# Parameter rows on GpSimd's queue, and the first quarter of scale multiplied between the transposes of x

## The chip, the core and the metric

The program runs on one core of one Trainium2 chip. The metric is the device time of one execution in microseconds (us); lower is better. TensorE (PE) multiplies, VectorE (DVE), ScalarE (ACT) and GpSimd (POOL) work on tiles, and SyncE (SP) only asks for transfers. ACT and GpSimd can ask for transfers too. Each engine works through its own list of instructions in order and waits on semaphores for the others.

## The reference

One layer of a flow-matching backbone on 512 latent tokens and 128 context tokens, 2048 wide, all in float32. What matters here is its beginning:

```python
sh1, sc1, g1, sh2, sc2, g2 = jnp.split(mod, 6, axis=-1)      # mod = silu(c) @ w_mod + b_mod
h = _rmsnorm(x, lp['norm1_g']) * (1.0 + sc1) + sh1
p = h @ lp['w_in']
o_a, s_fin = _rwkv7_bidir(shift_fn(p[..., :C_SHIFT], lp['mu_shift']), s0, lp)
o_b = _chunk_gmlp(jax.nn.gelu(p[..., C_SHIFT:]), lp)
x = x + g1 * (jnp.concatenate([o_a, o_b], axis=-1) @ lp['w_out'])
h = _rmsnorm(x, lp['norm2_g']) * (1.0 + sc2) + sh2
ff = (jax.nn.silu(h @ lp['w_ffn_gate']) * (h @ lp['w_ffn_up'])) @ lp['w_ffn_down']
return x + g2 * ff, s_fin
```

`mod` is computed for two conditioning vectors (latent and context) with w_mod of 2048 x 12288. `_rwkv7_bidir` reads small parameter vectors: mu_shift, w0, a0, k_k, k_a, r_k, gn_w and gn_b. After the layer comes a last RMSNorm.

## The kernel before

The 640 tokens stand as 5 tiles of 128 rows. The program has an opening of some 149 us, which makes the normalized and modulated h for all tokens, and then the main part: the rest of h @ w_in with the recurrence, w_out, the feed-forward products and the last norm. Only the opening's code is touched.

In the opening, each tile of x (`xall`) is squared and summed on ACT; GpSimd takes the reciprocal root `rs` (line 135); DVE scales the tile by it (line 242); TensorE transposes it in 16 blocks into the PSUM tile `ptx` (line 246); DVE and ACT copy it to `xnT` (line 247). TensorE's list is written out by hand in this stretch: its instructions stand in the order of the Python code. The other engines' lists are ordered by a scheduler from the same code.

Then come four rounds j = 0 to 3. Round j makes 512 columns of scale (g = 1) and 512 of shift (g = 0) of `mod`, each by `quarter(g, j)`. A quarter fetches four pieces of w_mod of 1 MB (`wt`, line 304, asked for by SyncE) and multiplies each with the conditioning vectors (`cT`, line 308, into `pm`, four products a piece; the trace counts each of them twice). Counted through all rounds, the pieces are called wt0 to wt31 here: wt0 to wt3 are the first quarter of scale. There are five buffers for them, so a piece can be asked for only when the product of the piece five before it is done. After the fourth piece ACT copies `pm` to `ms` (line 312), TensorE transposes `ms` in four blocks (`ptm`, line 316), and DVE reduces this to `mc`. After both quarters DVE makes `hf` (line 342) of four blocks of h, and splits it into `h_hi` and `h_lo` (lines 344 and 345). Between the pieces of the next round stand the first products of h with three column blocks of w_in (`products(j)`, lines 188 to 190, into `big`), whose weights are fetched as `raw` (line 165) and split into `hi` and `lo`.

```python
for j in range(4):
    for i, _ in enumerate(itertools.chain(quarter(1, j), quarter(0, j))):
        if i in (2, 3, 4, 6, 7, 8):
            next(prods, None)
    ...
    prods = products(j)
    if j == 1:
        rows()
    if j == 2:
        params()
```

`rows()` (lines 263 to 278) asks for 20 small transfers, of 128 bytes to 12 KB each, that put the parameter vectors as rows into `rowA` and `rowB`. `params()` (lines 280 to 286) transposes both on TensorE and copies the columns into `prm`, which the main part reads. `rowC` holds b_mod and norm1_g; ACT asks for it, and its transposition `pp` (line 250) gives `bmod` (line 252).

SyncE's list of the transfers follows the code. Besides the buffers, a transfer also waits for the landing of the one that was asked for eight before it on its kind of queue: SyncE and ACT share eight such lanes, called DMAHW0 to DMAHW7 in the lists of waits, and GpSimd has eight of its own, DMASW0 to DMASW7.

Of the kernel before, what the change touches and what calls it, by code (L numbers as in the profile page):

```python
# [22 lines left out]
T = 640  # L23
NT = T // P
HALF = T // 2
# [11 lines left out]
RMS_EPS = 1e-6  # L37
# [18 lines left out]
ROWO = 4  # L56
RAWB = 13
FRONT = 4
REST = 6
LATE = 2  # L60
OFF = 13
# [19 lines left out]
NPRM = 212  # L81
# [6 lines left out]
def flow_step(ctx: ExitStack, tc, x_prompt, x_sample, state_rwkv, c, c_ctx, w_mod, b_mod,  # L88
# [3 lines left out]
    nc = tc.nc  # L92
    V, S, G, TE = nc.vector, nc.scalar, nc.gpsimd, nc.tensor
# [19 lines left out]
    ident = cp.tile([P, P], F32, name="ident")  # L113
    make_identity(nc, ident)
    I2 = cb.tile([P, CH], F32, name="I2")
    for h in range(2):
# [8 lines left out]
                         op0=ALU.mult, op1=ALU.add)  # L125
# [8 lines left out]
    def rsqrt(out, in_):  # L134
        return G.tensor_tensor(out=out, in0=in_, in1=mhalf.to_broadcast(list(in_.shape)), op=ALU.pow)

    prm = cp.tile([P, NPRM], F32, name="prm")
# [57 lines left out]
    hpool = hp.enter_context(tc.tile_pool(name="hpool", bufs=1))  # L195
    junk = hpool.tile([P, D], F32, tag="h_hi", name="junk")
    xall = hpool.tile([P, NT, D], F32, tag="h_lo", name="xall")


    pmx, pex, pbx = ExitStack(), ExitStack(), ExitStack()  # L200
    pm_ = pmx.enter_context(tc.tile_pool(name="pm_", bufs=1, space=PSUM))
    ptE = pex.enter_context(tc.tile_pool(name="ptE", bufs=1, space=PSUM))
    FIRST = (3072, 3200, 3328)
    with ExitStack() as ph:
        ph.enter_context(tc.manual_schedule(engines={mybir.EngineType.PE}))
        p0 = ph.enter_context(tc.tile_pool(name="p0", bufs=1))
# [24 lines left out]
        V.tensor_copy(cT3[:, :, 1], pc[:, 0, 16:32])  # L231


        xnT = p0.tile([P, KB, T], F32, name="xnT")
        for t in range(NT):
            xt = xall[:, t, :]
            ss = p0b.tile([P, 1], F32, name="ss")
            S.activation(junk, xt, AF.Square, accum_out=ss)
            V.tensor_scalar(ss, ss, 1.0 / D, RMS_EPS, op0=ALU.mult, op1=ALU.add)
            rs = p0b.tile([P, 1], F32, name="rs")  # L240
            rsqrt(rs, ss)
            V.tensor_scalar_mul(xt, xt, rs[:, 0:1])
            for q in range(4):
                pt = ps0.tile([P, 4, P], F32, tag="pt", name="ptx")
                for b in range(4):
                    TE.transpose(pt[:, b, :], xt[:, (4 * q + b) * P:(4 * q + b + 1) * P], ident)
                (S.copy if q % 2 else V.tensor_copy)(xnT[:, 4 * q:4 * q + 4, t * P:(t + 1) * P], pt)

        pp = ps0.tile([P, 4, P], F32, tag="pt", name="pp")
        TE.transpose(pp[:, 0, 0:48], rowC, ident[0:48, 0:48])  # L250
        bmod = p0.tile([P, 2, KB], F32, name="bmod")
# [1 line left out]
        V.tensor_scalar_add(bmod[:, 1, :], bmod[:, 1, :], 1.0)  # L253
        V.tensor_copy(prm[:, C_N1:C_N2], pp[:, 0, 32:48])


        rowA = p0.tile([P, P], F32, name="rowA")
        rowB = p0.tile([P, P], F32, name="rowB")
        G.memset(rowB, 0.0)
        G.memset(rowA, 0.0)  # L260
        nA = C_W0

        def rows():
            for m in range(4):
                nc.sync.dma_start(rowA[C_MU + 24 * m:C_MU + 24 * m + 24, :],
                                  mu_shift[0, m, 0:3072].rearrange("(r p) -> r p", p=P))
                nc.sync.dma_start(rowA[C_MU2 + 2 * m:C_MU2 + 2 * m + 2, :],
                                  mu_shift[0, m, 3072:3328].rearrange("(r p) -> r p", p=P))
                nc.sync.dma_start(rowA[C_MU3 + m:C_MU3 + m + 1, 0:32], mu_shift[0, m:m + 1, 3328:3360])
            for off, src in ((C_W0, w0[0].rearrange("d (r p) -> (d r) p", p=P)),  # L270
                             (C_A0, a0[0].rearrange("d (r p) -> (d r) p", p=P)),
                             (C_KK, k_k[0].rearrange("(r p) -> r p", p=P)),
                             (C_KA, k_a[0].rearrange("(r p) -> r p", p=P)),
                             (C_RK, r_k[0].rearrange("(r h) n -> r (h n)", h=2)),
                             (C_GW, gn_w[0].rearrange("(r h) n -> r (h n)", h=2)),
                             (C_GB, gn_b[0].rearrange("(r h) n -> r (h n)", h=2)),
                             (C_N2, norm2_g[0].rearrange("(r p) -> r p", p=P))):
                nc.sync.dma_start(rowB[off - nA:off - nA + src.shape[0], :], src)

        def params():  # L280
            pp = ptE.tile([P, 4, P], F32, tag="ptE", name="pp")
            TE.transpose(pp[:, 0, :], rowA, ident)
            TE.transpose(pp[:, 1, :], rowB, ident)
            V.tensor_copy(prm[:, 0:nA], pp[:, 0, 0:nA])
            V.tensor_copy(prm[:, nA:C_N1], pp[:, 1, 0:C_N1 - nA])
            V.tensor_copy(prm[:, C_N2:NPRM], pp[:, 1, C_N2 - nA:NPRM - nA])

        psx.close()
        h_hi = hpool.tile([P, KB, T], F32R, tag="h_hi", name="h_hi")
        h_lo = hpool.tile([P, KB, T], F32R, tag="h_lo", name="h_lo")  # L290
        pe = pex.enter_context(tc.tile_pool(name="pe", bufs=6, space=PSUM))
        early = [[pe.tile([P, HALF], F32, tag="big", name="big") for _ in range(2)] for _ in FIRST]
        mc = p0.tile([P, 2, KB, 2], F32, name="mc")

        bc = lambda ap: ap.unsqueeze(2).to_broadcast([P, 4, 2])
# [1 line left out]
        def quarter(g, j):  # L297


            pm = pm_.tile([P, 512], F32, tag="pmod", name=f"pm{g}")  # L300
            V.memset(pm, 0.0)
            for q in range(4):
                wt = wmp.tile([P, 4, 512], F32, tag="wmod", name="wt")
                nc.sync.dma_start(wt, w_mod[0, 512 * q:512 * q + 512, g * D + 512 * j:g * D + 512 * j + 512]
                                  .rearrange("(i p) n -> p i n", p=P))
                for i in range(4):
                    k = 2 * (4 * q + i)
                    TE.matmul(pm[32 * i:32 * i + 2, :], cT[:, k:k + 2], wt[:, i, :],
                              start=(q == 0), stop=(q == 3), tile_position=(0, 32 * i))
                yield  # L310
            ms = p0b.tile([P, 512], F32, tag="ms", name=f"ms{g}")
            S.copy(ms, pm)
            yield
            pt = ptE.tile([P, 4, P], F32, tag="ptE", name="ptm")
            for cb in range(4):
                TE.transpose(pt[:, cb, :], ms[:, cb * P:(cb + 1) * P], ident)
            m = mc[:, g, 4 * j:4 * j + 4, :]
            V.tensor_reduce(out=m, in_=pt.rearrange("p cb (i r) -> p cb r i", r=32)[:, :, 0:2, :],
                            axis=AX.X, op=ALU.add)
            V.tensor_tensor(out=m, in0=m, in1=bc(bmod[:, g, 4 * j:4 * j + 4]), op=ALU.add)  # L320
            if g == 1:
                V.tensor_tensor(out=m, in0=m, in1=bc(prm[:, C_N1 + 4 * j:C_N1 + 4 * j + 4]), op=ALU.mult)

        def products(j):
            for col, halves in zip(FIRST, early):
                hi, lo = split(w_in[0, j * 512:(j + 1) * 512, col:col + P], 4)
                for hf in range(2):
                    win(halves, j, hi, lo, (hf,))
                    yield
# [1 line left out]

        prods = iter(())
        for j in range(4):
            for i, _ in enumerate(itertools.chain(quarter(1, j), quarter(0, j))):
                if i in (2, 3, 4, 6, 7, 8):
                    next(prods, None)
            for _ in prods:
                pass
            for kb in range(4 * j, 4 * j + 4):
                hf = p0b.tile([P, T], F32, name="hf")  # L340
                for (lo, hi, v) in SEG:
                    V.tensor_scalar(hf[:, lo:hi], xnT[:, kb, lo:hi], mc[:, 1, kb, v:v + 1],
                                    mc[:, 0, kb, v:v + 1], op0=ALU.mult, op1=ALU.add)
                S.copy(h_hi[:, kb, :], hf)
                V.tensor_sub(h_lo[:, kb, :], hf, h_hi[:, kb, :].bitcast(F32))  # L345
            prods = products(j)
            if j == 1:
                rows()
            if j == 2:
                params()  # L350
        for _ in prods:
            pass
# [1005 lines left out]
    rs = rsp.tile([P, T], F32, tag="rs2", name="rs2")  # L1358
# [36 lines left out]
    with ExitStack() as ph:  # L1395
# [8 lines left out]
        ss = [pss.tile([P, HALF], F32, name=f"ss{hf}") for hf in range(2)]  # L1404
# [365 lines left out]
    for f in range(2, NFF):  # L1770
        b = {n: [WB.pop((f, n, q)) for q in range(2)] for n in ("11", "12", "21", "22")}
# [217 lines left out]
```

## Time and profile before

| what | us |
|---|---|
| median of 3 runs | 3312.3 |
| lowest and highest run | 3306.03, 3312.47 |
| the profiled execution, its time | 3317.92 |
| its span from the first to the last instruction | 3316.1 |
| TensorE busy in the span | 3151.8 |
| VectorE, ScalarE, GpSimd busy | 2409.3, 1452.3, 1278.7 |

The times of instructions below are those of the profiled execution, counted from the start of its span. A row of a timeline gives the start, the time taken, the engine, the line of the kernel, the operation with the tile it writes and the tiles it reads, how many stand in the row, and in brackets how long the engine stood idle before it and what ended that. "SPq" and "ACTq" rows are requests for transfers; their time is that of asking. A row of a tile's view gives the shortest, median and longest of its instructions in nanoseconds. A row of stretches gives for each engine the busy time and the count, then TensorE's granted clock as a share of full speed, the busy share of the transfer engines and what they moved in GB/s.

### The profile page before, as it was taken

What the parts mean: (1) busy time and instruction counts of PE and PEld (TensorE: products, weight loads), DVE (VectorE), ACT (ScalarE), POOL (GpSimd) and SP (SyncE); (2) the same over time, 40 slices, a digit from 0 to 9 for tenths busy, and PEclk for the clock granted to TensorE, in tenths of its full rate; (3) what the DMA queues carried; (4) which work ended last, traced back from release to release, by engine and by line L of the source; (5) the groups of instructions that cost most, each with busy time, mean ns of one, the idle gap of its engine ahead of it and who ended that gap; (6) DMA issues with size and microseconds to landing.
All of it is one profiled execution on the core that took longest, in us unless ns stands there. A gap on an engine that the chain in (4) does not pass through costs nothing.

```text
span 3316.1 us, 72388 instructions
## 1 busy us (share of the span) xinstructions
PE 3151.8 (95%) x28216; PEld 2912.2 (88%) x28216; DVE 2409.3 (73%) x4152; ACT 1452.3 (44%) x3163; POOL 1278.7 (39%) x1114
## 2 busy tenths in 40 slices
PE   6899999999999999998999999999999999999996
PEld 3688788778877888888999999999999999999996
DVE  4448767766866677767877777877778787877787
ACT  3334444444443444334644444444444445444365
POOL 0001122222212113333155655656656555555543
PEclk8899999999999999999999999999999999999998
DMA  8767676767667488735534343443443454553453
GB/s 318 247 180 212 184 203 186 184 182 202 187 179 217 129 273 272 237 118 158 166 103 123 118 121 118 120 128 108 125 127 103 129 185 150 162 156 116 139 162 118
DMA packets 740142, 550.88 MB, mean 166 GB/s; under 512 B 140712, under 2 KB 673208, under 8 KB 730968
## 3 DMA queue, kind: packets, MB, share of 16 engines
q1 hardware_dynamic: 727480, 532.57, 53.7%
q0 software_dynamic: 9984, 13.13, 1.7%
q8 instruction: 222, 3.64, 0.5%
q14 instruction: 120, 0.98, 0.1%
q10 hardware_dynamic: 2336, 0.57, 0.1%
HBM read 437.79 MB, written 110.95 MB: 165 GB/s over the span
## 4 chain that ended last, share of the span: by engine, by line
PE 74%; DVE 10%; DMA 6%; issue 5%; POOL 3%; ACT 2%; SPq 0%; DVEq 0%; ACTq 0%; POOLq 0%
PE P L1604 15%; PE P L1603 15%; PE P L1602 15%; PE big L188 4%; PE big L190 4%; PE big L189 4%; PE pG L636 2%; PE pm L881 2%; DMA raw<-in_w_in_dram 2%; DMA wt<-in_w_mod_dram 1%; PE big L1013 1%; DVE lo L1392 1%; PE big L1449 1%; PE big L1447 1%; PE big L1448 1%
## 5 line engine op out<-in xcount | busy, mean ns | idle before, releaser
L1602 PE MATMUL P<-xo,hi 128*128 128x320 f32 x2352 | 728.2, 310 | 3.3 <-ACT hi L1391 3.3
L1604 PE MATMUL P<-xo,lo 128*128 128x320 f32 x2352 | 728.3, 310 | 2.0 <-DVE lo L1392 1.9
L1603 PE MATMUL P<-xo,hi 128*128 128x320 f32 x2352 | 728.1, 310 | 0.0
L1392 DVE TENSOR_TENSOR lo<-raw,hi 128x512 fp32r<-128x512 f32 x532 | 513.7, 969 | 169.1 <-ACT hi L1391 164.5
L1391 ACT CAST hi<-raw 128x512 fp32r<-128x512 f32 x532 | 330.7, 622 | 496.8 <-PE P L1603 389.7
L188 PE MATMUL big<-h_hi,hi 128*128 128x320 f32 x1376 | 452.3, 329 | 8.4 <-ACT hi L166 4.9
L1602 PEld LDWEIGHTS P<-xo,hi 128*128 128x128 f32 x2352 | 442.7, 188 | 3.5 <-ACT hi L1391 3.5
L1604 PEld LDWEIGHTS P<-xo,lo 128*128 128x128 f32 x2352 | 442.6, 188 | 2.8 <-DVE lo L1392 2.8
L1603 PEld LDWEIGHTS P<-xo,hi 128*128 128x128 f32 x2352 | 442.6, 188 | 0.0
L190 PE MATMUL big<-h_hi,lo 128*128 128x320 f32 x1376 | 435.1, 317 | 1.3 <-DVE lo L167 1.3
L189 PE MATMUL big<-h_lo,hi 128*128 128x320 f32 x1376 | 435.0, 316 | 0.7 <-DVE h_lo L345 0.7
L1515 POOL TENSOR_TENSOR raw<-raw 128x512 f32<-128x512 f32 x252 | 407.7, 1627 | 14.9 <-DVE lo L1392 3.3
L1604 PE MATMUL P<-xd,lo 128*128 128x320 f32 x1232 | 383.5, 311 | 14.0 <-DVE lo L1392 13.9
L1602 PE MATMUL P<-xd,hi 128*128 128x320 f32 x1232 | 382.0, 310 | 2.7 <-ACT hi L1391 0.9
L1603 PE MATMUL P<-xd,hi 128*128 128x320 f32 x1232 | 380.6, 309 | 0.0
L167 DVE TENSOR_TENSOR lo<-raw,hi 128x512 fp32r<-128x512 f32 x268 | 187.2, 701 | 218.9 <-ACT hi L166 214.8
L188 PEld LDWEIGHTS big<-h_hi,hi 128*128 128x128 f32 x1376 | 263.7, 192 | 75.7 <-issue 48.3
L166 ACT CAST hi<-raw 128x512 fp32r<-128x512 f32 x268 | 165.9, 619 | 274.7 <-PE big L189 124.4
L1391 ACT CAST hi<-rawd 128x512 fp32r<-128x512 f32 (+1 forms) x288 | 168.9, 587 | 241.5 <-PE P L1603 196.3
L189 PEld LDWEIGHTS big<-h_lo,hi 128*128 128x128 f32 x1376 | 264.3, 192 | 7.0 <-issue 3.5
L190 PEld LDWEIGHTS big<-h_hi,lo 128*128 128x128 f32 x1376 | 263.7, 192 | 7.5 <-DVE lo L167 3.0
L1604 PEld LDWEIGHTS P<-xd,lo 128*128 128x128 f32 x1232 | 231.2, 188 | 20.4 <-DVE lo L1392 19.9
(378 smaller groups left out, 6270.0 us busy)
## 6 DMA issues: line engine op xcount, KB each, us to landing
wt<-in_w_mod_dram SPq DMA_DIRECT2D x96, 1024.0 KB
raw<-in_w_ffn_gate_dram SPq DMA_DIRECT2D x182, 256.0 KB
raw<-in_w_ffn_up_dram SPq DMA_DIRECT2D x182, 256.0 KB
rec<-d_S SPq DMA_DIRECT2D x80, 576.0 KB
raw<-in_w_in_dram SPq DMA_DIRECT2D x172, 256.0 KB
rawd<-in_w_ffn_down_dram SPq DMA_DIRECT2D x128, 256.0 KB
raw<-in_w_out_dram SPq DMA_DIRECT2D x96, 256.0 KB
xd<-d_os SPq DMA_DIRECT2D x66, 320.0 KB
```

Source lines behind the costliest of these rows:

```text
L166: S.copy(hi, raw)
L167: V.tensor_sub(lo, raw, hi.bitcast(F32))
L188: TE.matmul(halves[hf], hi[:, k, :], h_hi[:, kb, s], start=(kb == 0), stop=False)
L189: TE.matmul(halves[hf], hi[:, k, :], h_lo[:, kb, s], start=False, stop=False)
L190: TE.matmul(halves[hf], lo[:, k, :], h_hi[:, kb, s], start=False, stop=(kb == KB - 1))
L636: TE.matmul(two[h][:, cc - c0, :], XZ[:, cc, h, :, :].rearrange("p s t -> p (s t)"), R[:, cc, :, :].rearrange("p s t -> p (s t)"), start=T ...
L1391: S.copy(hi[:, 0:nk], raw[:, 0:nk])
L1392: V.tensor_sub(lo[:, 0:nk], raw[:, 0:nk], hi[:, 0:nk].bitcast(F32))
L1515: G.tensor_tensor(out=o[:, 0:nk], in0=p[:, 0:nk], in1=q[:, 0:nk], op=ALU.subtract)
L1602: TE.matmul(ps, hi[:, k, :], xk[:, 0, :], start=f, stop=False)
L1603: TE.matmul(ps, hi[:, k, :], xk[:, 1, :], start=False, stop=False)
L1604: TE.matmul(ps, lo[:, k, :], xk[:, 0, :], start=False, stop=l)
```

## The change

`rows()` now asks through GpSimd's queue, and is called right after the five tiles of x. The generator of the first quarter of scale, `lead`, is made before the tiles, and is advanced by one piece after each tile from the third (`BEGIN = 2`) on, so that wt0, wt1 and wt2 are multiplied after tiles 2, 3 and 4. The transposition of `rowC` stands ahead of x. `params()` is called at the end of round 1. The rest of the first quarter and everything behind it keep their order.

```diff
+BEGIN = 2
...
-        xnT = p0.tile([P, KB, T], F32, name="xnT")
-        for t in range(NT):
...
         pp = ps0.tile([P, 4, P], F32, tag="pt", name="pp")
         TE.transpose(pp[:, 0, 0:48], rowC, ident[0:48, 0:48])
...
         def rows():
             for m in range(4):
-                nc.sync.dma_start(rowA[C_MU + 24 * m:C_MU + 24 * m + 24, :],
+                nc.gpsimd.dma_start(rowA[C_MU + 24 * m:C_MU + 24 * m + 24, :],
...
-                nc.sync.dma_start(rowB[off - nA:off - nA + src.shape[0], :], src)
+                nc.gpsimd.dma_start(rowB[off - nA:off - nA + src.shape[0], :], src)
...
+        lead = quarter(1, 0)
+        xnT = p0.tile([P, KB, T], F32, name="xnT")
+        for t in range(NT):
...
+                (S.copy if q % 2 else V.tensor_copy)(xnT[:, 4 * q:4 * q + 4, t * P:(t + 1) * P], pt)
+            if t >= BEGIN:
+                next(lead)
+        rows()
...
-            for i, _ in enumerate(itertools.chain(quarter(1, j), quarter(0, j))):
+            for i, _ in enumerate(itertools.chain(lead if j == 0 else quarter(1, j), quarter(0, j))):
...
             if j == 1:
-                rows()
-            if j == 2:
                 params()
```

TensorE's list at the start of the program, before (a trailing x16 stands for 16 alike, four pieces of wt):

```order
L227 MATMUL pc<-ident,crow 128x32
L246 MATMUL ptx<-ident,xall 128x128 x80
L250 MATMUL pp<-ident,rowC 128x48
L308 MATMUL pm_322<-wt,cT 2x512 x16
L316 MATMUL ptm<-ident,ms_348 128x128 x4
```

All 80 transposes of the five tiles stand ahead of the first product with wt. The same place now:

```order
L228 MATMUL pc<-ident,crow 128x32
L236 MATMUL pp<-ident,rowC 128x48
L309 MATMUL ptx<-ident,xall 128x128 x48
L257 MATMUL pm_250<-wt,cT 2x512 x4
L309 MATMUL ptx<-ident,xall 128x128 x16
L257 MATMUL pm_250<-wt,cT 2x512 x4
L309 MATMUL ptx<-ident,xall 128x128 x16
L257 MATMUL pm_250<-wt,cT 2x512 x8
L265 MATMUL ptm<-ident,ms_368 128x128 x4
```

wt0 stands behind tile 2, wt1 behind tile 3, and wt2 and wt3 behind tile 4.

SyncE's list between the last piece of round 1 (wt15) and the first rows, before, with what each waits for:

```order
L304 DMA wt<-in_w_mod_dram 128x4x512 [waits DMAHW4_49,PE_49]
L265 DMA rowA<-in_mu_shift_dram 24x128 [waits DMAHW5_49,Pool_49]
L267 DMA rowA<-in_mu_shift_dram 2x128 [waits DMAHW6_49]
L269 DMA rowA<-in_mu_shift_dram 1x32 [waits DMAHW7_49]
L265 DMA rowA<-in_mu_shift_dram 24x128 [waits DMAHW0_49]
L267 DMA rowA<-in_mu_shift_dram 2x128 [waits DMAHW1_49]
L269 DMA rowA<-in_mu_shift_dram 1x32 [waits DMAHW2_49]
L265 DMA rowA<-in_mu_shift_dram 24x128 [waits DMAHW3_49]
L267 DMA rowA<-in_mu_shift_dram 2x128 [waits DMAHW4_49]
```

The same place now holds wt15, wt16, wt17 and wt18, and then `raw`:

```order
L253 DMA wt<-in_w_mod_dram 128x4x512 [waits DMAHW4_49,PE_49]
L253 DMA wt<-in_w_mod_dram 128x4x512 [waits DMAHW6_49,DMAHW5_49,PE_49]
L253 DMA wt<-in_w_mod_dram 128x4x512 [waits DMAHW0_49,PE_49]
L253 DMA wt<-in_w_mod_dram 128x4x512 [waits DMAHW7_49,DMAHW1_49,PE_49]
L166 DMA raw<-in_w_in_dram 128x4x128 [waits DVE_49]
```

The 20 rows are gone from SyncE's list; before, the eighth of them waited for the lane of wt15.

GpSimd's list between the second and the fourth root, where nothing stood between the roots before:

```order
L136 TENSOR_TENSOR rs<-ss,mhalf 128x1 [waits DVE_49]
L281 DMA rowA<-in_mu_shift_dram 24x128
L283 DMA rowA<-in_mu_shift_dram 2x128 [waits DMASW0_49]
L285 DMA rowA<-in_mu_shift_dram 1x16x2 [waits DMASW1_49]
L281 DMA rowA<-in_mu_shift_dram 24x128 [waits DMASW2_49]
L283 DMA rowA<-in_mu_shift_dram 2x128 [waits DMASW3_49]
L285 DMA rowA<-in_mu_shift_dram 1x16x2 [waits DMASW4_49]
L136 TENSOR_TENSOR rs<-ss,mhalf 128x1 [waits DVE_49,Pool_49]
L294 DMA rowB<-in_a_dram 16x128 [waits DMASW5_49]
L294 DMA rowB<-in_k_k_dram 8x128 [waits DMASW6_49]
L294 DMA rowB<-in_k_a_dram 8x128 [waits DMASW7_49]
```

Ahead of the first root shown stand seven more rows behind the root of tile 0; behind the last row shown stand three more ahead of the fourth root, and one between the fourth and the fifth. From the ninth row on each waits for the lane of the row eight before it.

More of the change, by code (lines that the diff above doesn't have):

```diff
@@ L231, in flow_step @@
         V.tensor_copy(cT3[:, :, 1], pc[:, 0, 16:32])
-        xnT = p0.tile([P, KB, T], F32, name="xnT")
-        for t in range(NT):
[L236 to L247, printed above, removed]
         pp = ps0.tile([P, 4, P], F32, tag="pt", name="pp")
@@ L254, in flow_step @@
         V.tensor_copy(prm[:, C_N1:C_N2], pp[:, 0, 32:48])
[L257 to L292, printed above, removed]
         mc = p0.tile([P, 2, KB, 2], F32, name="mc")
@@ new lines, in flow_step @@
+        lead = quarter(1, 0)
+        xnT = p0.tile([P, KB, T], F32, name="xnT")
+        for t in range(NT):
+            xt = xall[:, t, :]
+            ss = p0b.tile([P, 1], F32, name="ss")
+            S.activation(junk, xt, AF.Square, accum_out=ss)
+            V.tensor_scalar(ss, ss, 1.0 / D, RMS_EPS, op0=ALU.mult, op1=ALU.add)
+            rs = p0b.tile([P, 1], F32, name="rs")
+            rsqrt(rs, ss)
+            V.tensor_scalar_mul(xt, xt, rs[:, 0:1])
+            for q in range(4):
+                pt = ps0.tile([P, 4, P], F32, tag="pt", name="ptx")
+                for b in range(4):
+                    TE.transpose(pt[:, b, :], xt[:, (4 * q + b) * P:(4 * q + b + 1) * P], ident)
+                (S.copy if q % 2 else V.tensor_copy)(xnT[:, 4 * q:4 * q + 4, t * P:(t + 1) * P], pt)
+            if t >= BEGIN:
+                next(lead)
@@ new lines, in flow_step, with params @@
+        rows()
+        def params():
+            pp = ptE.tile([P, 4, P], F32, tag="ptE", name="pp")
+            TE.transpose(pp[:, 0, :], rowA, ident)
+            TE.transpose(pp[:, 1, :], rowB, ident)
+            V.tensor_copy(prm[:, 0:nA], pp[:, 0, 0:nA])
+            V.tensor_copy(prm[:, nA:C_N1], pp[:, 1, 0:C_N1 - nA])
+            V.tensor_copy(prm[:, C_N2:NPRM], pp[:, 1, C_N2 - nA:NPRM - nA])
+        psx.close()
+        h_hi = hpool.tile([P, KB, T], F32R, tag="h_hi", name="h_hi")
@@ L324, in products @@
+        h_lo = hpool.tile([P, KB, T], F32R, tag="h_lo", name="h_lo")
+        pe = pex.enter_context(tc.tile_pool(name="pe", bufs=6, space=PSUM))
+        early = [[pe.tile([P, HALF], F32, tag="big", name="big") for _ in range(2)] for _ in FIRST]
         def products(j):
```

19 lines of the change are left out of this document (added).

## The prediction

> **What bounds the kernel now.** I read the page first, then the granted clock and busy time by stretches, then the timelines of TensorE, SyncE and GpSimd up to 150 us.
>
> ```profile
> PE   6899999999999999998999999999999999999996
> DMA  8767676767667488735534343443443454553453
> ```
>
> In the forty slices of the span (83 us each), TensorE is full from the third to the last but one, while the transfer engines are far from full there. Time can be won in the first two, where TensorE still waits; what the opening wins or loses is carried to the end by a TensorE that has no slack. The next view cuts the opening at the four-block transposes that close each of its rounds (round 0 ends at 45.69, round 1 at 71.24, round 2 at 103.61, round 3 at 130.51).
>
> ```profile
> core 0: us, PE busy (x) PEld busy (x) DVE busy (x) ACT busy (x) POOL busy (x), PEclk, DMA share, GB/s
> 45.69:71.24 25.55, 22.34 (x144) 12.83 (x145) 10.39 (x23) 5.75 (x9) 0.00 (x0) 0.94 0.85 297
> 71.24:103.61 32.37, 24.01 (x147) 13.05 (x145) 9.99 (x22) 5.91 (x9) 0.00 (x0) 0.84 0.98 346
> 103.61:130.51 26.90, 23.63 (x148) 14.40 (x146) 11.01 (x27) 6.94 (x11) 1.65 (x2) 0.87 0.89 300
> ...
> 28.70:33.20 4.50, 4.50 (x45) 2.27 (x46) 1.83 (x6) 1.17 (x2) 0.00 (x0) 1.00 0.16 29
> 65.80:73.80 8.00, 5.69 (x40) 4.11 (x36) 3.03 (x8) 1.40 (x3) 0.00 (x0) 1.00 0.11 25
> ```
>
> Rounds 2 and 3 hold the same work (147 and 148 products), yet round 2 takes 32.37 us and round 3 26.90. And twice the transfer engines, otherwise saturated near 380 GB/s, fall to 29 and 25 GB/s: for 4.5 us from 28.7 and for 8.0 us from 65.8. Each hole has its cause in the order of the queues. The first, on TensorE's and SyncE's timelines:
>
> ```profile
> 12.23 3.68 PE L246 MATMUL ptx<-ident,xall 128*128 128x128 f32 x16 [3.23 <-DVE xall L242]
> ...
> 20.22 1.94 PE L246 MATMUL ptx<-ident,xall 128*128 128x128 f32 x16 [1.11 <-DVE xall L242]
> 24.67 3.29 PE L246 MATMUL ptx<-ident,xall 128*128 128x128 f32 x16 [2.51 <-ACT junk L238]
> 28.36 1.99 PE L246 MATMUL ptx<-ident,xall 128*128 128x128 f32 x16 [0.39 <-DVE xall L242]
> ...
> 30.46 3.62 PE L308 MATMUL pm<-wt,cT 128*2 128x512 f32 x32
> ...
> 35.45 1.04 PE L308 MATMUL pm<-wt,cT 128*2 128x512 f32 x8
> ...
> 43.09 1.89 PE L308 MATMUL pm<-wt,cT 128*2 128x512 f32 x8 [2.52 <-DMA wt<-in_w_mod_dram]
> ...
> 31.56 7.03 SPq L304 DMA_DIRECT2D wt<-in_w_mod_dram  x6
> ```
>
> Five wt buffers are asked for early (wt0 to wt4); wt5 needs wt0's buffer back, and wt0 is multiplied only after all transposes of x, at 30.46. So SyncE asks for wt5 at 31.56, when the stream has been dry since 28.7. TensorE pays: it waits 2.52 us before wt7 at 43.09. The second hole, on SyncE's timeline:
>
> ```profile
> 54.78 2.50 SPq L304 DMA_DIRECT2D wt<-in_w_mod_dram  x1
> 57.38 1.16 SPq L265 DMA_DIRECT2D rowA<-in_mu_shift_dram  x1
> ...
> 61.13 0.23 SPq L267 DMA_DIRECT2D rowA<-in_mu_shift_dram  x1
> 64.47 0.22 SPq L269 DMA_DIRECT2D rowA<-in_mu_shift_dram  x1
> 65.33 0.30 SPq L265 DMA_DIRECT2D rowA<-in_mu_shift_dram  x1
> 67.97 0.23 SPq L267 DMA_DIRECT2D rowA<-in_mu_shift_dram  x1
> ...
> 72.00 0.32 SPq L278 DMA_DIRECT2D rowB<-in_norm_g_dram  x1
> 72.42 1.49 SPq L304 DMA_DIRECT2D wt<-in_w_mod_dram  x3
> ```
>
> and in the waits of SyncE's queue between 56 and 74 us (total, times, longest):
>
> ```profile
> SPq L269 <- DMA wt<-in_w_mod_dram: 3.1, 1, 3.1
> SPq L267 <- DMA wt<-in_w_mod_dram: 3.0, 2, 2.3
> ```
>
> Behind wt15 (issue over at 57.28) stand the 20 rows, and wt16 comes behind them at 72.42. Each transfer waits for the one eight before it on its kind of queue, so the eighth row (67.97) cannot go before wt15 has landed: that empties the stream. Then twelve issues at 0.25 to 0.41 us each pass before wt16. Its buffer had long been free:
>
> ```profile
> 55.86 1.04 PE L308 MATMUL pm<-wt,cT 128*2 128x512 f32 x8
> ...
> 77.79 1.89 PE L308 MATMUL pm<-wt,cT 128*2 128x512 f32 x8 [5.95 <-DVE h_lo L345]
> ```
>
> wt11, whose buffer it takes, was done at 56.9. TensorE then idles 5.95 us before wt16 at 77.79. (The view names DVE, but this product reads only wt and cT; wt16, asked for at 72.42, is the late one.)
>
> **The change part by part.** First, the early products. wt0 is multiplied behind the transposes of tile 2, which end at 20.22 + 1.94 = 22.16; a group takes 3.62 / 4 = 0.9; with 1 us for a later GpSimd (below), wt5 can be asked for at 24.1, before the stream runs dry at 28.7. A transfer of 1.05 MB at 0.38 MB a us takes 2.75, so wt5 fills the stream to 31.45. wt1 follows tile 3 (27.96 + 1 + 0.9 = 29.9); from asking to first bytes took 31.56 to 33.2 = 1.6, so wt6 starts at 31.5, no hole. wt2 follows tile 4 (30.35 + 1 + 1.8 = 33.1), wt7 starts at 34.7 and ends at 37.4. Before, wt5 to wt7 ran from 33.2 to 41.45. **Saved: 4.0 us**, at most the hole of 4.5.
>
> Second, the rows leave SyncE. wt16 now follows wt15 without a hole, since wt11's buffer is free. On the old clock it would land near 70, before TensorE wants it at 71.8; wt18 lands near 76 against a wish at 74, a wait like the one round 3 has. So round 2 becomes like round 3, which has no rows in its queue: 32.37 - 26.90 = **5.5 saved**. Bounds: 8.0, the whole hole, if TensorE could follow the stream; and nothing, if DVE was the true wait at 77.79. I take 5.5, because TensorE's chain (mc, h, products at the lower clock of 0.84 to 0.87) is the same in both rounds.
>
> Third, params() moves from round 2's end to round 1's end with its two transposes and three copies:
>
> ```profile
> 104.53 0.30 PE L282 MATMUL pp<-ident,rowA 128*128 128x128 f32 x1 [0.33 <-issue]
> 106.10 0.26 DVE L284 COPY prm<-pp 128x108 f32<-128x108 f32 x1
> ```
>
> Under 1 us changes its place, and both places lie behind a wait: nothing. The rows are wanted at about 67 on the new clock (71.24 - 4.0) and are asked for before 30. The transposition of rowC goes ahead of x, where TensorE waited 3.23 us for tile 0, and its three small DVE operations go with it into that pause: nothing.
>
> Fourth, what GpSimd pays. Its reciprocal roots rs, one for each tile of x, now stand behind row issues: 7 ahead of the second, 6 each ahead of the third and fourth, 1 ahead of the fifth.
>
> ```profile
> 10.28 0.57 POOL L135 TENSOR_TENSOR rs<-ss,mhalf 128x1 f32<-128x1 f32 x1 [8.76 <-DVE ss L239]
> 14.21 0.57 POOL L135 TENSOR_TENSOR rs<-ss,mhalf 128x1 f32<-128x1 f32 x1 [3.21 <-DVE ss L239]
> 18.20 0.55 POOL L135 TENSOR_TENSOR rs<-ss,mhalf 128x1 f32<-128x1 f32 x1 [3.42 <-DVE ss L239]
> 22.66 0.55 POOL L135 TENSOR_TENSOR rs<-ss,mhalf 128x1 f32<-128x1 f32 x1 [3.90 <-DVE ss L239]
> ...
> L672 POOL DMA_DIRECT2D dd<-GB x128: 537/537/786, 231.3 to 1048.3; - x128
> ...
> DMA to landing us min/median/max: 1.8/3.4/7.3
> ```
>
> GpSimd idles 3.2 to 3.9 us between two roots. An issue takes 0.54 (the largest 0.79): from 10.85, seven take 4.1, root two starts at 14.95 instead of 14.21; six more (3.3) bring root three to 18.8 instead of 18.20, and root four to 22.7. From the ninth issue on each also waits for the landing of the one eight before: with the median of 3.4 this costs nothing, with 5.2 (what crow took under a full stream)
>
> ```profile
> 1.18 5.20 DMA crow<-in_c_ctx_dram
> ```
>
> root four comes 1.2 late. I take 1 us, already in the first term. Below nothing is excluded: an added issue cannot make a root earlier.
>
> A rule of the Trainium skill speaks against this part: SBUF — State Buffer ("SBUF: two separate sides", its box on DVE blocking DMA) says that GpSimd cannot write descriptors while VectorE runs a two-port operation. By it each tile's scaling of x, which follows its root at once, would hold the row issues for its length, three times ahead of root four, which would come 3.7 late; the first term would fall by 1 and the time be 3303.8.
>
> ```profile
> L242 DVE TENSOR_SCALAR xall<-xall,rs x5: 1285/1286/1287, 10.9 to 26.9; 128x2048 f32<-128x2048 f32 x5
> ```
>
> No row of this trace shows a GpSimd issue held by such an operation: the 128 issues of dd lie between 537 and 786 ns.
>
> The sum: 4.0 + 5.5 = 9.5. The profiled execution took 3317.9 (its span of 3316.1 and 1.8 around it) and would take 3308.4; the median of the runs, 3312.3, lies 5.6 below it, so the forecast is **3302.8**.
>
> **The rivals.**
> The roots come late (0.13). If a row under the full stream lands after L us, root four stands behind three turns of eight, at about 13.5 + 2L; x ends 5 us behind it (an issue, root five, 1.3 of scaling and 2 of transposes), and wt7's group ends 7.4 behind that: two groups of 0.9 left, 1.4 to the next product (34.08 to 35.45) and four of 1.04. Before, that group ended at 43.09 + 1.89 = 45.0. So at L = 9.5 the first term is gone: 3312.3 - 5.5 = 3306.8. For it: the largest landing of dd, 7.3, was under a stream less than full. Against: the median 3.4.
>
> Slower (0.10): the same place, GpSimd's root four behind lanes that wait for landings, with a larger price. From L = 12.3 on both terms are eaten (13.5 + 24.6 + 12.4 = 50.5, 5.5 behind the old 45.0). At L = 18 the group ends at 61.9, 16.9 late: 3312.3 + 16.9 - 5.5 = 3323.7. Against it stands that 18 is 2.5 times the longest landing shown.
>
> The rows were hidden (0.10): the wait of 5.95 us at 77.79 was for DVE, as the view says, and wt16 asked for earlier changes nothing. Then only the first term is left: 3308.3. Against it: the stream was dry for 8.0 us, and what is named does not feed that product.
>
> DMA: Bandwidth & Descriptors of the Trainium skill (Issuing engines are not separate DMA queues) points the same way: issuing from several engines saves only the sequencer's time, usually small. Here the trace disagrees: the rows held SyncE from 57.38 to 72.42.
>
> Given back (0.05): the main part starts 9.5 us earlier and waits for a transfer there: 3312.3. Against it: TensorE's nines, with transfer shares of 0.3 to 0.7.
>
> **How the numbers follow.** The forecast has the remaining 0.62. About 0.2% (6.6 us; the three runs shown spread over 6.4) can be told from no change. Faster by more: 0.58 of the forecast's and half of the late roots' and a little else, 0.66. Within: 0.24, the rest of these, the hidden rows and the given back. Slower: 0.10. The range goes down to 3296, where both holes close (4.5 + 8.0 = 12.5, so 3299.8) and a run falls 4 us low, and up to 3313, past the cases at 3307, 3308 and 3312; it leaves out the slower case and some tails.
>
> **What would show it.** Right: no fall of the transfer rate near 28 and 66 us; wt7's group near 39; round 2 near 27 us long; the fourth root near 23 to 24; and the opening's last stretch some 9.5 us earlier with everything behind it shifted alike. Wrong in the first term: roots more than 3 us late, or idle time on GpSimd put down to its row transfers. Wrong in the second: round 2 still above 30 us with a full stream, DVE's h being the wait. Wrong altogether: an opening shortened by 9 us and an end that is not.

## Result and profile after

The changed kernel takes 3298.7 us (median of 12 runs, 3290.4 to 3310.0) against 3309.4 for the kernel before (12 runs on the same chip, 3301.3 to 3313.0): 10.7 us or 0.3% less. The ratio of the two sets of runs is 0.9971 with a 95% interval from 0.9961 to 0.9981, which by itself is 9.6 us, with an interval from 6.3 to 12.9. The forecast was 3302.8, a gain of 9.5.

The profiled execution of the changed kernel took 3294.6 us, with a span of 3292.8. Its difference to the profiled execution before, 23.3 us of span, isn't the change alone: the opening (up to the first product of the main part) ends at 136.84 instead of 149.00, 12.2 earlier, and the main part took 3156.0 instead of 3167.1. A second profiled execution of the changed kernel took 3164.9 there, so the other 11 us are the spread of one execution against another. What the change does has to be read from the opening.

In the page of the changed kernel, TensorE's and the transfer engines' rows of the forty slices:

```profile
PE   6999999999998999998899999999999999999996
DMA  9666776766667588645533433433433454553453
```

The first slice of the transfer engines is now a 9, TensorE's second a 9. The view of stretches, cut at the same four-block transposes (rounds 0 to 3, then the rest of the opening), and below it the two stretches that were dry before:

```profile
0.00:41.26 41.26, 21.89 (x150) 13.26 (x151) 16.99 (x41) 17.89 (x24) 17.80 (x35) 0.96 0.98 369
41.26:67.89 26.63, 22.96 (x144) 13.94 (x145) 10.48 (x23) 5.85 (x9) 0.00 (x0) 0.87 1.06 377
67.89:92.34 24.45, 20.97 (x148) 12.83 (x146) 10.22 (x26) 5.81 (x9) 0.00 (x0) 1.00 1.06 375
92.34:118.63 26.29, 22.72 (x146) 13.82 (x144) 10.71 (x23) 6.94 (x11) 1.65 (x2) 0.87 0.88 296
118.63:136.84 18.21, 14.50 (x78) 12.97 (x75) 15.04 (x40) 9.72 (x19) 3.13 (x5) 0.81 0.51 148
...
65.80:73.80 8.00, 6.16 (x46) 2.92 (x42) 5.68 (x16) 2.96 (x5) 0.00 (x0) 1.00 1.06 374
28.70:33.20 4.50, 4.50 (x42) 2.15 (x40) 3.31 (x5) 1.76 (x3) 0.00 (x0) 1.00 1.05 382
```

The last column is GB/s. Where it was 29 and 25, it is 382 and 374, and the stream stays full to the end of round 2. Round 0 ends 4.4 earlier than before (45.69), round 2 is 7.9 shorter (32.37), round 1 is 1.1 longer. The same in the transfer view of 20 to 80 us, forty slices of 1.5 us each, first the kernel before:

```profile
GB/s 382 389 388 385 386 291 11 0 96 350 404 401 391 381 385 386 386 386 388 362 353 383 338 383 388 384 393 368 343 381 202 25 4 15 13 62 287 410 403 386
```

and the changed one:

```profile
GB/s 382 377 371 385 379 381 367 388 382 381 384 392 388 382 385 389 382 340 379 351 365 387 386 385 388 350 361 387 388 386 385 389 386 347 366 371 354 380 386 396
```

From such a row a dry time can be added up: for each slice under 330 GB/s, the 1.5 us times the share that is missing from 384. It is 12.6 us before (4.5 and 8.1) and nothing now.

TensorE's timeline of the changed kernel, at the early products, before wt7 and before wt16:

```profile
22.45 3.33 PE L309 MATMUL ptx<-ident,xall 128*128 128x128 f32 x16 [2.99 <-DVE ss L302]
25.71 1.26 PE L257 MATMUL pm<-wt,cT 128*2 128x512 f32 x8
26.97 1.94 PE L309 MATMUL ptx<-ident,xall 128*128 128x128 f32 x16
28.84 1.04 PE L257 MATMUL pm<-wt,cT 128*2 128x512 f32 x8
...
39.52 1.04 PE L257 MATMUL pm<-wt,cT 128*2 128x512 f32 x8 [1.67 <-DMA wt<-in_w_mod_dram]
...
69.40 1.90 PE L257 MATMUL pm<-wt,cT 128*2 128x512 f32 x16
```

wt7 is multiplied at 39.52 (43.09 before). wt16, for which TensorE idled 5.95 us, comes without a wait at 69.40. But tile 2's transposes end at 25.78 and not at the 22.16 that the prediction reckoned with. They take 3.33 us instead of 1.94, and they start 2.2 us late. GpSimd's timeline shows the reason for the late start:

```profile
10.36 0.57 POOL L136 TENSOR_TENSOR rs<-ss,mhalf 128x1 f32<-128x1 f32 x1 [8.68 <-DVE ss L302]
10.93 1.42 POOL L294 DMA_DIRECT2D rowB<-in_w_dram  x1
12.35 0.56 POOL L281 DMA_DIRECT2D rowA<-in_mu_shift_dram  x1
...
15.46 0.59 POOL L136 TENSOR_TENSOR rs<-ss,mhalf 128x1 f32<-128x1 f32 x1
16.00 1.47 POOL L281 DMA_DIRECT2D rowA<-in_mu_shift_dram  x1
17.47 0.51 POOL L283 DMA_DIRECT2D rowA<-in_mu_shift_dram  x1
...
20.41 0.58 POOL L136 TENSOR_TENSOR rs<-ss,mhalf 128x1 f32<-128x1 f32 x1
20.93 1.47 POOL L294 DMA_DIRECT2D rowB<-in_a_dram  x1
...
24.93 0.58 POOL L136 TENSOR_TENSOR rs<-ss,mhalf 128x1 f32<-128x1 f32 x1
25.45 1.47 POOL L294 DMA_DIRECT2D rowB<-in_norm_g_dram  x1
```

The roots two, three and four stand at 15.46, 20.41 and 24.93; before, at 14.21, 18.20 and 22.66. A row issue takes 0.50 to 0.56 us, but the one behind each root takes 1.42 to 1.47.

### The profile page after: what moved, and what is told of

Its sections match the earlier page's. It is cut to its first block, busy times and chain, and to the rows that moved or that the text cites. A ratio compares the mean times of both kernels' runs of the same rounds, so it can differ in the third digit from the quotient of the medians.

```text
span 3292.8 us, 72403 instructions
## 1 busy us (share of the span) xinstructions
PE 3138.9 (95%) x28216; PEld 2906.2 (88%) x28216; DVE 2393.1 (73%) x4152; ACT 1451.3 (44%) x3163; POOL 1291.9 (39%) x1134
## 4 chain that ended last, share of the span: by engine, by line
PE 76%; DVE 9%; issue 6%; POOL 4%; DMA 3%; ACT 2%; SPq 0%; DVEq 0%; POOLq 0%; ACTq 0%
PE P L1608 15%; PE P L1606 15%; PE P L1607 15%; PE big L189 5%; PE big L190 4%; PE big L191 4%; PE pG L640 2%; PE pm L885 2%; DMA raw<-in_w_in_dram 1%; PE big L1453 1%; PE big L1451 1%; PE big L1452 1%; PE big L1017 1%; PE pblk L824 1%; DVE mx L785 1%
## 5 line engine op out<-in xcount | busy, mean ns | idle before, releaser
L1396 DVE TENSOR_TENSOR lo<-raw,hi 128x512 fp32r<-128x512 f32 x532 | 504.7, 952 | 179.7 <-ACT hi L1395 174.6
L168 DVE TENSOR_TENSOR lo<-raw,hi 128x512 fp32r<-128x512 f32 x268 | 187.5, 702 | 203.0 <-ACT hi L167 194.7
```

The lines of the kernel that those rows point to most:

```text
L168: V.tensor_sub(lo, raw, hi.bitcast(F32))
L1396: V.tensor_sub(lo[:, 0:nk], raw[:, 0:nk], hi[:, 0:nk].bitcast(F32))
```

## The experiments

The theory for them: TensorE follows the stream of weights through rounds 0 to 2, so the opening ends at what a full stream allows, plus the time for which the stream is dry. What a part of the change is worth is the dry time that it takes away. The rivals are those of the prediction, and a price of the late roots. This table holds all that was measured: the start of wt0's product, the dry time from 20 to 80 us, the end of the opening in the profiled execution, and the ratio of its times to those of the kernel before, with its interval. Each kernel was profiled once, not all on one chip; the two that were profiled a second time have both openings in the table.

| kernel | wt0 at | dry, us | opening ends | ratio |
|---|---|---|---|---|
| before; once more | 30.46; 30.55 | 12.6; 12.9 | 149.00; 147.77 | 1 |
| the change; once more | 25.71; 25.57 | 0; 0 | 136.84; 139.01 | 0.9971 [0.9961, 0.9981] |
| rows alone | 33.41 | 7.3 | 147.03 | 1.0000 [0.9985, 1.0015] |
| rows alone, behind the roots | 30.30 | 4.3 | 141.50 | 0.9987 [0.9977, 0.9998] |
| early products alone | 21.81 | 7.8 | 144.62 | 0.9992 [0.9982, 1.0002] |
| both, rows behind the roots | 21.75 | 0 | 137.18 | 0.9967 [0.9953, 0.9981] |
| early products, no rows at all | 21.63 | 0 | 138.23 | 0.9979 [0.9967, 0.9992] |
| early products, seven rows on SyncE | 21.77 | 3.6 | 139.40 | 0.9980 [0.9968, 0.9991] |
| early products, rows on ScalarE | 22.36 | 3.7 | 141.42 | 0.9986 [0.9975, 0.9996] |
| the change, BEGIN = 1 | 19.32 | 0 | 136.36 | 0.9974 [0.9965, 0.9984] |
| the change, BEGIN = 3 | 29.70 | 3.7 | 142.79 | 0.9981 [0.9968, 0.9993] |
| the change, rows twice | 25.53 | 0.8 | 139.25 | 0.9968 [0.9957, 0.9980] |

The five openings without dry time end at 136.4 to 139.0, 137.5 in the mean. Each of the others lies at 137.5 plus its dry time, within 2.6 us; so the openings can't place a dry time of 1 or 2 us. The intervals of the ratios are 6 to 10 us wide, so single parts are told apart by the openings, and those only where they differ by more than the 1 to 2 us between two executions of one kernel. All diffs below are against the changed kernel.

**Before and the change once more.** Both unaltered.

> The kernel before once more, unaltered, for the spread of the opening from one execution to the next: the opening ends at 149.0 within 1.0, with both dry stretches (4.5 and 8.0 us).

> The changed kernel once more, unaltered: the opening ends at 136.8 within 1.0, without a dry stretch.

Measured 147.77 and 139.01; both miss their margin, by 0.2 and 1.2. The opening is worth 12.2 us by the first pair of profiles and 8.8 by the second, 10.5 in the mean, close to the 10.7 of the medians. Most of what the changed kernel's second execution lost is in round 2, by the view of stretches:

```profile
67.67:93.67 26.00, 22.53 (x149) 13.40 (x147) 10.22 (x26) 5.81 (x9) 0.00 (x0) 0.93 1.06 376
```

26.00 us at a granted clock of 0.93 instead of 24.45 at 1.00, for the same work and a stream as full. And round 3 of the kernel before, in its second execution:

```profile
104.06:128.51 24.45, 20.83 (x149) 12.72 (x146) 11.04 (x27) 6.94 (x11) 1.66 (x2) 1.00 0.97 329
```

24.45 at 1.00, where the first showed 26.90 at 0.87.

**The two parts apart.**

```diff
-BEGIN = 2                     # rows alone
+BEGIN = 5
```

> Rows by GpSimd and the earlier parameter transposes alone; all products of scale behind all transposes of x, as before. The stream theory (TensorE follows the transfers through rounds 0 to 2, so each closed hole is won at its length): the first hole stays, 1.3 us longer because the fifth root comes 1.3 us late; the second (8.0) goes. Rounds 1 and 2 together near 51, the opening ends near 149.0 + 1.3 - 7.5 = 142.8, ratio near 0.998. The prediction's sizing (round 2 becomes like round 3, 5.5): opening ends near 144.8, ratio 0.9987. Rival, the rows were hidden and the wait at 77.79 was DVE's: round 2 stays above 30 us, the opening ends near 150.3, ratio 1.000.

```diff
-                nc.gpsimd.dma_start(...)     # early products alone: all 20 rows
+                nc.sync.dma_start(...)
...
-        rows()                # behind the tiles of x
...
             if j == 1:
+                rows()
+            if j == 2:
                 params()
```

> Early products alone; the 20 rows stay on SyncE behind wt15, their transposes at the end of round 2. Stream theory and prediction alike: the first hole goes, wt7's group near 39, the opening ends 4.4 earlier, near 144.6, ratio near 0.9986; the second hole stays, 7 to 8 us long, with 5 to 6 us of waiting before wt16 and a round 2 of 31 to 32.5. Rival, what was won early is only handed on to the next wait (SyncE meets the rows earlier but TensorE waits for something else): the opening still ends near 149, ratio 1.000.

The early products alone come out as expected: 144.62, with the second hole in its old place (transfer view from 20 us, slices of 1.5 us) and TensorE's wait for wt16 behind it, this time put down to the transfer:

```profile
GB/s 388 390 384 388 389 385 385 382 384 391 382 382 386 391 385 388 364 354 383 336 377 389 389 385 381 340 376 240 29 8 13 13 74 307 406 403 381 392 345 373
```

```profile
73.11 1.89 PE L257 MATMUL pm<-wt,cT 128*2 128x512 f32 x8 [4.93 <-DMA wt<-in_w_mod_dram]
```

The rows alone do not: the opening ends at 147.03 and the median doesn't move, where 142.8 was expected. The second hole is gone, but the first is 7.3 us long instead of 4.5:

```profile
GB/s 378 370 381 382 377 386 83 11 0 0 55 279 406 404 388 380 389 386 386 388 385 376 341 386 343 373 388 385 389 385 339 374 384 386 391 385 386 386 337 380
```

TensorE's timeline says why. wt0 waits for the transposes of tile 4, and these started at 29.84 and took 3.65 us:

```profile
29.84 3.65 PE L309 MATMUL ptx<-ident,xall 128*128 128x128 f32 x16 [1.10 <-DVE xall L305]
33.41 4.02 PE L257 MATMUL pm<-wt,cT 128*2 128x512 f32 x32
```

and by the view of stretches TensorE ran there at a granted clock of 0.50, with 5 GB/s coming in:

```profile
30.00:33.50 3.50, 3.50 (x20) 3.17 (x23) 1.67 (x3) 0.59 (x1) 0.00 (x0) 0.50 0.02 5
```

That leaves two readings: the late roots took what the rows had won, or something else did.

**The rows behind the roots.** GpSimd's list in this phase is taken as written, which puts all 20 issues behind the fifth root; once with the early products and once without (there `BEGIN` is 5 as well).

```diff
-        ph.enter_context(tc.manual_schedule(engines={mybir.EngineType.PE}))
+        ph.enter_context(tc.manual_schedule(engines={mybir.EngineType.PE, mybir.EngineType.Pool}))
```

> Both parts, with GpSimd's instructions of this phase in written order, so all 20 row issues stand behind the fifth root. The roots return to 14.2, 18.2, 22.7, 26.3. Theory that the descriptors of a row wait for VectorE's scaling: of the 20 issues only the first, behind the fifth root, takes 1.4 us, all others 0.50 to 0.56. Stream theory: the 2.3 us by which the fourth root came late in the change cost nothing, because the stream stays full either way: opening ends at 136.8 within 0.6, ratio 0.997. Rival, the late roots were paid for: opening ends near 134.5, ratio 0.996.

> Rows alone on GpSimd, but all 20 issues behind the fifth root; no early products. It tells why the rows alone won only 2.0 us of the opening (147.03). Theory that the late roots took the rest there: with the roots back at 14.3, 17.9, 22.3, 24.7 the last transposes of x end near 29.2, wt0 follows at once (33.41 with the rows between the roots), the first hole is 3 to 4 us and the second is gone: the opening ends between 140.5 and 142.5. Rival, the late roots are not what cost it (the clock of TensorE, or the rows' own transfers): the opening ends at 146 to 147 again.

Without early products the opening ends at 141.50, inside the expected 140.5 to 142.5, with the first hole back at 4.3 us. On TensorE's timeline wt0 is 3.1 us earlier than with the rows between the roots:

```profile
28.44 1.94 PE L309 MATMUL ptx<-ident,xall 128*128 128x128 f32 x16 [1.64 <-DVE xall L305]
30.30 3.62 PE L257 MATMUL pm<-wt,cT 128*2 128x512 f32 x32
```

Of these 3.1 us, 1.4 is the fifth root (26.42 instead of 27.81) and 1.7 the slower transposes (1.94 instead of 3.65). Round 0 is 3.3 shorter. The slower transposes are the granted clock, 0.50 there and 1.00 here by the view of stretches; that the late roots brought the low clock is not shown. So of the 5.5 us between the two openings 3.3 belong to round 0, 1.4 of them to the late root and the rest to the clock; the other 2.2 lie in the rounds behind and are no more than two executions of one kernel differ by. The ratios of the two kernels, 1.0000 and 0.9987, overlap in their intervals and don't tell them apart. With the early products, the same move wins nothing that can be told: 137.18 against 136.84 and 139.01, ratio 0.9967 against 0.9971. The late roots are covered there.

On the long issues: GpSimd's timeline with the rows behind the roots, and both early parts, has one among 20.

```profile
24.68 0.55 POOL L136 TENSOR_TENSOR rs<-ss,mhalf 128x1 f32<-128x1 f32 x1 [1.81 <-DVE ss L302]
25.26 1.39 POOL L281 DMA_DIRECT2D rowA<-in_mu_shift_dram  x1
26.65 0.53 POOL L283 DMA_DIRECT2D rowA<-in_mu_shift_dram  x1
```

It might be long for coming behind a root. The kernel with the rows alone excludes that; there DVE was busy when root three was done and scaled the tile late, by DVE's timeline:

```profile
20.82 1.28 DVE L305 TENSOR_SCALAR xall<-xall,rs 128x2048 f32<-128x2048 f32 x1
```

and by GpSimd's timeline the issue behind the root is short, and the next is long:

```profile
20.44 0.54 POOL L294 DMA_DIRECT2D rowB<-in_a_dram  x1
20.98 1.21 POOL L294 DMA_DIRECT2D rowB<-in_k_k_dram  x1
```

An issue that falls into DVE's scaling of x ends 0.1 us after the scaling does (22.10 and 22.19 here). The issue behind the root had begun 0.38 us before the scaling, while DVE copied `ptx` out of PSUM (20.21 to 20.90), and was not held.

**No rows at all.**

```diff
-        rows()                # behind the tiles of x
```

> Early products, and the 20 rows left out altogether (rowA and rowB stay zero, so parameters are left out of the computation). What remains of the rows' price in the change shows against it. Stream theory: the opening ends within 1 us of the change's 136.8, ratio 0.997: the rows cost nothing any more on GpSimd. Rival, their 0.3 MB and the late roots still cost: 2 us earlier or more, below 134.8, ratio 0.996.

The opening ends at 138.23, 0.4 beyond the expected margin and between the two executions of the change. (The rows add up to 0.1 MB, not 0.3.) On GpSimd's queue the rows cost nothing that these profiles can show.

**Seven rows on SyncE.**

```diff
-            for m in range(4):            # rowA's twelve rows
+            for m in range(0):
...
-                             (C_N2, norm2_g[0]...)):       # the last of rowB's eight
-                nc.gpsimd.dma_start(rowB[...], src)
+                nc.sync.dma_start(rowB[...], src)
...                                       # rows() and params() placed as in "early products alone"
```

> Early products; of the 20 rows only seven stay, at their old place on SyncE behind wt15, and the other 13 are left out of the computation. It tells waits for turns from issue time. Theory that each transfer waits for the landing of the one eight before: wt16 is now the eighth behind wt15 and is asked for when wt15 lands, near 63, instead of 67.76 with 20 rows; a dry stretch of 2 to 4 us remains, and the opening ends near 140 (144.62 with 20 rows, 136.84 with none). Rival, SyncE's time for the issues is the price: 7 x 0.3 = 2 us, wt16 is asked for near 55.5, no dry stretch, opening at 137.

SyncE's timeline, the seventh row and wt16 to wt18:

```profile
60.69 0.27 SPq L293 DMA_DIRECT2D rowB<-in_gn_b_dram  x1
63.37 1.49 SPq L253 DMA_DIRECT2D wt<-in_w_mod_dram  x3
```

and the waits of its queue from 53 to 65 us, where line 253 is that of wt (total, times, longest):

```profile
SPq L253 <- DMA wt<-in_w_mod_dram: 2.4, 1, 2.4
```

wt16 is asked for at 63.37, not at 55.5, and it is a landing that held it. Of the 10.1 us from the first row (53.29) to wt16, SyncE's issues are 4.5 and its waits for landings 5.4. The stream is dry for 3.6 us, and the opening ends at 139.40. Seven rows already empty the stream, and by the turns of eight: without the waits wt16 would have been asked for near 58, and the stream runs dry only behind 60.5 (an estimate from these rows); the other thirteen hold wt16 4.4 us longer (67.76).

**The rows on ScalarE.**

```diff
-                nc.gpsimd.dma_start(...)      # all 20 rows
+                nc.scalar.dma_start(...)
```

> Early products, and the 20 rows on ScalarE's queue instead of GpSimd's, among its squares and copies of x. Theory that any queue other than SyncE's will do as long as wt follows wt without a row between: roots undelayed but for ScalarE's own issues (20 x 0.3 = 6 us in its pauses), no dry stretch, the opening ends at 137 to 138.5. Rival, ScalarE's transfers share the turns of eight with SyncE's: rows wait for weights to land with ScalarE's copies of x behind them, x ends 3 to 10 us later and the opening ends at 140 to 147.

141.42, with 3.7 us dry: my theory that any queue but SyncE's would do falls. The rival named the right cause, shared turns, but the wrong victim. ScalarE's copies weren't late (x is transposed by 29.7); SyncE was. Its waits in the first 15 us:

```profile
SPq L214 <- DMA xall<-in_x_sample_dram: 4.3, 1, 4.3
SPq L253 <- DMA rowB<-in_a_dram: 2.7, 1, 2.7
SPq L214 <- DMA rowC<-in_norm_g_dram: 2.4, 1, 2.4
```

SyncE waits 2.7 us for the landing of a row that ScalarE asked for, and asks for wt0 at 12.21 instead of 6.46. That alone does not empty the stream, which still moves 336 GB/s from 18 to 24 us; from 24 to 28 it is 99. Most of the dry time comes from wt3. SyncE's waits from 20 to 32 us have 5.4 us for another row, and by its timeline wt3 is asked for only behind them:

```profile
SPq L253 <- DMA rowA<-in_mu_shift_dram: 5.7, 2, 5.4
```

```profile
25.71 0.37 SPq L253 DMA_DIRECT2D wt<-in_w_mod_dram  x1
```

**How much slack the early products have.**

```diff
-BEGIN = 2
+BEGIN = 1                     # and, in another kernel, 3
```

> The change with the early products beginning one tile earlier, behind the second tile of x, so that all four of the quarter stand among the transposes. Stream theory: the stream is already full to the end of round 2, so nothing is won: opening at 136.8 within 0.8, ratio as the change's. Rival, TensorE's own order is the limit of round 0: the round ends 1 to 2 us earlier than 41.26, the opening at 135 to 136.

> The change with the early products beginning one tile later, behind the fourth tile of x. It tells how much slack the early products have. In the change wt0 is multiplied at 25.71; here at about 28.8, 3.1 later, so wt5 is asked for 3.1 later. Theory that the request for wt5 sets the stream: it runs dry again for about 2.8 us from 28.7, and the opening ends near 139.6. Rival, any place among the transposes of x is early enough: no dry stretch, opening at 136.8.

A tile earlier wins nothing (136.36, and round 0 ends at 41.31), as the stream theory has it. A tile later costs more than expected: 142.79. wt0 came at 29.70, and the stream was dry for 3.7 us; round 0 is 3.2 longer, the rest is in the rounds behind. So the change stands near the edge: wt0's product at 25.71 is early enough, and 4.0 us later costs 3.7.

```diff
-        def rows():
+        def rows(rowA=rowA, rowB=rowB):
...
+        rows(p0.tile([P, P], F32, name="rowA2"), p0.tile([P, P], F32, name="rowB2"))   # rows twice
```

> The change with all 20 rows fetched a second time into two tiles that nothing reads. Five of the added issues stand ahead of the fifth root, the other fifteen behind it. It tries how late a root may come before the early products no longer cover it. Stream theory: root five comes 2 to 3 us later (27.64 in the change), the third early product with it, wt7 is asked for 2 to 3 us later, the stream runs dry for that time less 0 to 1 of slack, and the opening ends at 138 to 140. Rival, the early products cover any late root of this size: no dry stretch, opening at 136.8 to 137.2.

139.25 lies in the expected 138 to 140, but the change itself, the second time, ended at 139.01, so the opening decides nothing here. The stream does: the fifth root came 1.4 late (29.03), less than expected, one slice fell to 185 GB/s, and 0.8 us were dry. The third early product came 1.2 late (32.94 instead of 31.71). The slack behind the third early product is about half a microsecond.

No version beats the change by more than these measurements resolve; rows behind the roots is its equal, with roots that are not late.

## Why the prediction was right, and where it was not

**First term, early products: 4.0 forecast.** Measured 3.8 alone (the mean of the two openings before, 148.4, less 144.6), and 4.4 and 3.7 at the end of round 0. The size was right; the working behind it had errors that cost nothing by luck. It let wt5 be asked for at 24.1, which is 4.6 before the stream runs dry at 28.7. In fact wt0's product ended at 26.97, SyncE asked for wt5 at 27.04, and with the 1.6 from asking to first bytes wt5 arrived at about 28.6. Slack of nearly three microseconds was eaten by step four and by tile 2's transposes, 3.33 us instead of 1.94 (granted clock 0.55 there, 1.00 before). With wt1 two errors cancelled. Its product ended at 29.88, where 29.9 was forecast: root four came 1.3 later than allowed for, and tile 3's transposes took 1.94 instead of 3.29 (granted clock 1.00, 0.56 before). At which tile the clock is low stood in no term of the sum.

**Second term, the rows off SyncE: 5.5 forecast.** Measured 6.9 alone, with the roots undisturbed (148.4 less 141.5; 1.4 with the rows where the change has them), and 6.8 and 6.7 as the fall of rounds 1 and 2 together in the two pairs (57.92 to 51.08, 58.80 to 52.12). The mechanism was right: the eighth row waited for wt15, and the wait of 5.95 us at 77.79 was wt16's, not DVE's. The mis-sized step is "round 2 becomes like round 3": round 3's 26.90 was taken at a granted clock of 0.87, and TensorE's chain at that clock was no floor. The first bound, the hole of 8.0, was nearer.

**Third, params() and rowC: nothing.** `pp` now stands at 68.82 with an idle time of 0.33 ahead of it, as before. The move was not tried by itself.

**Fourth, GpSimd: 1 us at most forecast for root four.** It came 2.3 late (2.0 in the second execution). The issue price of 0.54 held for all but the one behind each root; the waits for landings, of which the 1 us was made, came to 0.4 us: two short pauses, ahead of the issues at 18.63 and 19.87, which by GpSimd's list wait for nothing but lanes (rows landed in 4.7 to 6.2 us, and eight issues with a root between take about as long). What failed is the step that weighed the page against "no row of this trace": the traces agree with SBUF — State Buffer of the Trainium skill (SBUF: two separate sides, its box on DVE blocking DMA). GpSimd's issue is held while DVE scales, 0.9 us at a time, three times ahead of root four: 2.8 more in issues, 2.3 in the root, against the 3.7 reckoned by it. That page of the Trainium skill gives "blocked until DVE-end + ~115 ns" (A bandwidth-pool intuition that's wrong); the traces show 0.09 to 0.10 us. The prediction took 1 off the first term for a root four that is 3.7 late. By its own figures it would be 2.7: it had wt6's first bytes at 31.5, just as wt5 ends, so all that root four is late beyond the 1 us allowed for would be dry time. With the 2.3 measured that is 1.3, and tile 3's faster transposes gave it back.

**The rivals.** Slower by late roots didn't happen, but its place was the right one: without the early products, the late roots and the low clock took 3.3 of the 6.9 that the rows are worth. The prediction added its two terms as if each stood alone; the sum held because one part covers the other's price. "Hidden rows" is excluded by 6.9 us. "Given back" is excluded as a whole, by runs that are 9.6 to 10.7 us faster, but not in part: over the eleven kernels of the table other than the one before, the ratios give 1.4 us less than the openings in the mean. DMA: Bandwidth & Descriptors of the Trainium skill (Issuing engines are not separate DMA queues), named with the first of these, says that issuing from several engines saves only the sequencer's time. The runs show more: moving the rows from SyncE to ScalarE still leaves 3.7 us dry, to GpSimd none, so here the choice of queue decides more than the sequencer's time: it decides for whose landings the next weight has to wait.

**The sum.** 9.5 forecast, 10.5 by the openings, 10.7 by the medians, 9.6 by the ratio; 3.8 and 6.9 of the parts alone, the rows behind the roots, add up to 10.7.

## What to carry to other kernels

Where a stream of large transfers bounds a stretch, look for the slices in which it is dry, and ask of each what the next request stood behind; the stretch shortens by the dry time, until TensorE's own chain is next. Small transfers don't cost their bytes or their issue time there but the landings that the requests behind them wait for, so they go to a queue with turns of its own, and behind whatever that engine owes to others. (Another place in SyncE's own list, ahead of wt0 or behind the last weight, might do as well; it was not tried.) Before a part of a change is judged useless alone, see whether the other part covers its price.

## What the runs showed of the hardware

- A row issue on GpSimd that meets DVE's scaling of a 128x2048 float32 tile (1.29 us) takes 1.21 to 1.47 us instead of 0.50 to 0.56, and ends 0.1 us after the scaling. Issues during DVE's copies out of PSUM were not held (0.50 at 19.14, within a copy from 19.06 to 19.75).
- SyncE's requests waited for landings of transfers that ScalarE had asked for (2.4, 2.7 and 5.4 us, with the rows on ScalarE); in the changed kernel no wait of SyncE for one of the 20 rows is seen up to 137 us.
- One and the same round took 24.45 us at a granted clock of 1.00, 26.00 at 0.93 and, with the rows alone, 26.74 at 0.87, with the stream at 375 to 376 GB/s each time. Two executions of one kernel differed by up to 2.2 us in the opening and 9 us in the main part; what makes the latter is not shown.
